# Both directions of a gated linear attention stacked on 128 partitions, with the backward states kept in DRAM

## The chip, the cores and the metric

The kernel runs on one core of a Trainium2 chip. The metric is the device time of one execution in microseconds (us); a kernel's time is the median of its runs. The engines are TensorE (PE; its weight loads are PEld), VectorE (DVE), ScalarE (ACT), GpSimd (POOL) and SyncE (SP), which here only issues DMAs.

## The reference, cut to what matters

One inference step of a two-layer hybrid backbone over 2048 latent tokens and a prompt of 128, model width 1024. The even layer runs a bidirectional gated linear attention (GLA, four heads, 64 key and 128 value channels each) beside a bidirectional S5 scan; the odd layer has windowed attention beside a short convolution. Shift, scale and gate of each layer come from a product with the conditioning vector (adaLN). The GLA of one direction:

```python
def step(S, inp):
    qc, kc, vc, gc = inp
    b = jnp.cumsum(gc, axis=2)
    o_inter = jnp.einsum('bhcd,bhde->bhce', qc * jnp.exp(b), S)
    diff = b[:, :, :, None, :] - b[:, :, None, :, :]
    decay = jnp.where(causal, jnp.exp(jnp.where(causal, diff, 0.0)), 0.0)
    att = jnp.einsum('bhid,bhjd,bhijd->bhij', qc, kc, decay)
    o = o_inter + jnp.einsum('bhij,bhje->bhie', att, vc)
    b_last = b[:, :, -1:, :]
    S_new = jnp.exp(b_last)[:, :, 0, :, None] * S + jnp.einsum('bhcd,bhce->bhde', kc * jnp.exp(b_last - b), vc)
    return S_new, o
```

It is run forward and on the flipped sequence, and both outputs are added: `o_f + fl(o_b)`. Each output chunk thus takes a forward state S (what came before it) and a backward state (what comes after it), each times the queries weighted by that direction's gates.

## The kernel before

Tokens are cut into 17 tiles of 128: 0 to 15 latent, 16 the prompt; a GLA chunk is one such tile. Tensors that pass between stages lie in DRAM (`qk_d`, `v_d`, `b_d` with the cumulated gates of both directions, `ys_d`, `zg_d`). A scheduler that simulates the engines sets the order of instructions on each engine from the program text, so an edit in one place can reorder engines elsewhere. Times are of the profile.

Start, 0 to 60 us. `ada` (L144) makes 512 columns of the adaLN vector: it loads a bias `bb` (L154) and eight weight tiles (L167), multiplies (L170), copies the sum out (L173), adds the bias (L175) and turns it into columns of shift or scale (L185 to L190). Four such units come first. `xt` are the token tiles (L278), `wst` weight tiles (L199) that are split in two parts for products of higher precision, `hf` and `ht` the normalized and modulated tokens and their parts (L245 to L249).

60 to 344 us: input projection (L341, L342) with the setup of S5 beside it. 344 to 715: S5 core, with parts of the projection (`qz_pass`) beside it.

Back stage, 715 to 900. `gla_back` (L890) walks over the tiles from the last to the first and makes every backward state; `zg_pass`, `glu_pass` (L816) and eight more adaLN units run beside it. `kv_update` (L921) turns the weighted keys (L926) and multiplies them with v (L932) for four heads, two on partitions 0 to 63 and two on 64 to 127. All 16 backward states stay in SBUF (`self.sb`, 16 KB per partition).

Crossing and chunks, 900 to 1340. `phase4` (L1132) weaves three chunks in flight: chunk i's attention, the turn of chunk i-1 and the output projection of chunk i-2 (`out_proj`, products into psD). `gla_pre` (L988) loads a chunk and makes `kh` and the queries `hq` weighted by the exponentiated gates (L1012), and steps the forward state (L1031). `gla_arg` (L964) makes the arguments of one of eight levels of the decay: four subtractions on GpSimd (L980 to L983; `q` of the last level on L972), an exponential on ScalarE (L984), a product on VectorE (L985); `gla_chunk` (L1034) multiplies them (L1058) and merges the levels (L1062, L1065). Then come three products per head into one PSUM tile: queries with the forward state (L1073) and with the backward state (L1074), each over 64 rows, and the attention with v (L1075). L1077 copies the result out, L1084 normalizes it.

1340 to 1850: the odd layer's projection and convolution; 1850 to 2422: attention.

Of the kernel before, what the change touches and what calls it, by code (L numbers as in the profile page):

```python
# [48 lines left out]
class Kernel:  # L49
# [55 lines left out]
    def setup(self, es):  # L105
# [33 lines left out]
        self.b_d = d.tile([2, 2, 128, NT], F32, name="b_d")  # L139
        self.z_d = d.tile([16, 512, 137], F32, name="z_d")  # L140
# [3 lines left out]
    def ada(self, l, j, wp, ring=None, bufs=4):  # L144
# [8 lines left out]
        bb = wp.tile([2, n], F32, name="bb", tag="ada_bb", bufs=bufs)  # L153
# [736 lines left out]
    def gla_back(self, es):  # L890

        nc, a = self.nc, self.a
        p = self.pool(es, "gbk", 2, side="left")
        for i in [16] + list(range(15, 0, -1)):
            ts = slice(i * 128, (i + 1) * 128)
            k = p.tile([128, 2, 128], F32, name="bk", tag="bk")
            B = p.tile([128, 2, 128], F32, name="bB", tag="bB")
            nc.sync.dma_start(k, self.qk_d[256:512, ts].rearrange("(r p) t -> p r t", p=128))
            nc.sync.dma_start(B, self.b_d[:, 1, :, ts].rearrange("r p t -> p r t"))
            v = p.tile([128, 512], F32, name="bv", tag="bv")  # L900
            nc.sync.dma_start(v, self.v_d[ts, :])
            E = p.tile([128, 2, 128], F32, name="bE", tag="bE")
            nc.gpsimd.tensor_tensor(E, B[:, :, 0:1].to_broadcast([128, 2, 128]), B, op=OP.subtract)
            nc.scalar.activation(E, E, AF.Exp, scale=0.0625)
            nc.vector.tensor_tensor(E, E, k, op=OP.mult)
            kv = self.kv_update(p, E, v)
            if i == 16:
                st = p.tile([128, 2, 128], F32, name="bst", tag="bst", bufs=1)
                nc.scalar.copy(st, kv)
                nc.sync.dma_start(self.o["gla"][1].rearrange("r p v -> p r v"), st)  # L910
                yield
                continue
            eb = p.tile([128, 2], F32, name="beb", tag="beb")
            nc.scalar.activation(eb, B[:, :, 0], AF.Exp, scale=0.0625)
# [6 lines left out]
    def kv_update(self, p, kd, v):  # L921
# [66 lines left out]
    def gla_pre(self, i):  # L988
# [7 lines left out]
        for j in range(2):  # L996
            nc.sync.dma_start(qk[:, j], self.qk_d[256 * j : 256 * j + 256, ts].rearrange("(r p) t -> p r t", p=128))
            nc.sync.dma_start(B[:, j], self.b_d[:, j, :, ts].rearrange("r p t -> p r t"))
        v = st["v"] = self.ga["v"].tile([128, 512], F32, name="v", tag="v", bufs=1)
# [10 lines left out]
        qh, st["att"] = (qa[:, 512 * j : 512 * j + 512].rearrange("p (a b c) -> p a b c", a=2, b=2) for j in range(2))  # L1010
        st["qh"] = qh
# [9 lines left out]
        sf = st["sf"] = self.sf  # L1021
        if i != 15:
            kv = self.kv_update(p, kh, v)
            if i == 16:
                o = p.tile([128, 2, 128], F32, name="fst", tag="sf", bufs=3)
                nc.scalar.copy(o, kv)
                nc.sync.dma_start(self.o["gla"][0].rearrange("r p v -> p r v"), o)
            else:
                self.sf = p.tile([128, 2, 128], F32, name="sf", tag="sf", bufs=3)
                for pr in range(2):  # L1030
                    V.scalar_tensor_tensor(self.sf[:, pr], sf[:, pr], eb[:, pr : pr + 1], kv[:, pr], op0=OP.mult, op1=OP.add)  # L1031
        yield

    def gla_chunk(self, i, out):  # L1034
# [4 lines left out]
        v, qh, sf = st["v"], st["qh"], st["sf"]  # L1039
# [28 lines left out]
        for h in range(4):  # L1068
            pr, hh = h // 2, h % 2
            o = 64 * hh  # L1070
# [498 lines left out]
    def run(self):  # L1569
        a = self.a  # L1570
        take = lambda g, n: [next(g, None) for _ in range(n)]
        with ExitStack() as es:
            self.setup(es)
            eW = es.enter_context(ExitStack())
            with ExitStack() as eA:
# [21 lines left out]
                c = self.pool(eR, "glac", 1, side="left")  # L1597
                self.sb = c.tile([128, 16, 2, 128], F32, name="sb")
                self.sf = c.tile([128, 2, 128], F32, name="sf0")
                self.nc.sync.dma_start(self.sb[:, 15], a["s0"][1])  # L1600
                self.nc.sync.dma_start(self.sf, a["s0"][0])
# [65 lines left out]
def prep(**z):  # L1667
# [56 lines left out]
        "s0": c_(n["state_gla"][0, 0].reshape(2, 2, 128, 128).transpose(0, 2, 1, 3)),  # L1724
# [51 lines left out]
```

## Time and profile before

| | |
|---|---|
| median of 3 runs | 2425.09 us (2424.18 to 2429.84) |
| profiled execution | 2423.86 us |
| its span | 2422.1 us |
| busy TensorE / VectorE / ScalarE / GpSimd | 2295.5 / 1720.3 / 986.2 / 872.9 us |
| moved by DMA | 303.92 MB |

The span is what the trace covers; the rest of the execution lies around it. Busy times are sums over the span, and TensorE's contains modelled ends. In a row of a timeline, the first number is the start in us, the second the duration of the group in us, `x2` the number of instructions in it; in square brackets stands how long the engine had waited and for what. TensorE's float32 products appear as two records each.

### The profile page before, as it was taken

The page shows a single profiled execution, that of the slowest core. Times are in us where ns is not written, and L with a number is a line of the kernel's source. Part 1 is how long each engine was busy: PE and PEld are TensorE (multiplying, and loading weights), DVE is VectorE, ACT ScalarE, POOL GpSimd, SP SyncE. Part 2 cuts the span into 40 slices and gives each one's busy share as a digit, 9 for nine tenths or more (in the row PEclk, how much of TensorE's full clock was granted, in tenths as well). Part 3 has the DMA queues.
Part 4 walks back from the last instruction along what each step waited for, and adds up shares of the span by engine and source line. Part 5 has one row for each costly group of instructions (what it writes and reads, how often), then busy time and mean ns, then how long its engine had stood idle before and what let it go on. Part 6 is the DMA issues. An engine that isn't in the chain of part 4 may idle for free.

```text
span 2422.1 us, 47150 instructions
## 1 busy us (share of the span) xinstructions
PE 2295.5 (95%) x17521; PEld 2110.7 (87%) x17521; DVE 1720.3 (71%) x3932; ACT 986.2 (41%) x2365; POOL 872.9 (36%) x1328
## 2 busy tenths in 40 slices
PE   7998998999999986999999999999999998999998
PEld 4987887777787875888888999999999997999998
DVE  5998689999976776888888675556344336676765
ACT  4553532222244453445554532233122115565653
POOL 4017047777612227666765022211001102222221
PEclk9999999999999995989999999999999998999999
DMA  8442552233269873333433642245124213222221
GB/s 303 153 141 79 170 159 78 80 82 96 81 202 315 294 242 112 122 105 114 124 118 99 192 135 79 79 134 169 50 73 122 68 56 113 88 88 88 89 70 57
DMA packets 313174, 303.92 MB, mean 125 GB/s; under 512 B 43696, under 2 KB 264464, under 8 KB 312944
## 3 DMA queue, kind: packets, MB, share of 16 engines
q1 hardware_dynamic: 255072, 227.70, 31.6%
q10 hardware_dynamic: 48112, 42.38, 5.4%
q0 software_dynamic: 9760, 30.83, 3.5%
q8 instruction: 138, 2.26, 0.4%
q14 instruction: 92, 0.75, 0.1%
HBM read 212.43 MB, written 88.39 MB: 124 GB/s over the span
## 4 chain that ended last, share of the span: by engine, by line
PE 53%; DVE 7%; issue 5%; DMA 4%; POOL 2%; ACT 2%; SPq 0%; ACTq 0%; POOLq 0%; DVEq 0%
PE psW L100 7%; PE psW L102 7%; PE psW L101 7%; PE psD L100 6%; PE psD L102 6%; PE psD L101 6%; PE psW L1487 2%; PE psW L1440 2%; PE psT L1475 2%; PE psP L1058 2%; PE psP L1075 1%; PE psP L1073 1%; DVE hq L1065 1%; DVE arg L985 1%; DVE yT L1103 1%
## 5 line engine op out<-in xcount | busy, mean ns | idle before, releaser
L100 PE MATMUL psD<-slot,yT 128*128 128x256 f32 x1088 | 316.4, 292 | 2.4 <-ACT yT L1102 2.4
L102 PE MATMUL psD<-slot,yT 128*128 128x256 f32 x1088 | 314.0, 292 | 0.4 <-DVE yT L1103 0.4
L101 PE MATMUL psD<-slot,yT 128*128 128x256 f32 x1088 | 311.2, 287 | 0.0
L101 PE MATMUL psW<-hq,slot 128*128 128x272 f32 x1024 | 293.0, 288 | 0.0
L102 PE MATMUL psW<-hq,slot 128*128 128x272 f32 x1024 | 292.9, 287 | 0.0
L100 PE MATMUL psW<-hq,slot 128*128 128x272 f32 x1024 | 289.1, 287 | 0.0
L101 PE MATMUL psD<-hq,slot 128*128 128x272 f32 x768 | 227.8, 297 | 14.5 <-DVE hq L230 14.5
L100 PE MATMUL psD<-hq,slot 128*128 128x272 f32 x768 | 230.0, 301 | 9.4 <-ACT fo L791 8.2
L102 PE MATMUL psD<-hq,slot 128*128 128x272 f32 x768 | 228.5, 298 | 0.0
L100 PEld LDWEIGHTS psD<-slot,yT 128*128 128x128 f32 x1088 | 208.0, 191 | 9.9 <-ACT yT L1102 2.8
L101 PEld LDWEIGHTS psD<-slot,yT 128*128 128x128 f32 x1088 | 208.1, 191 | 2.1
L102 PEld LDWEIGHTS psD<-slot,yT 128*128 128x128 f32 x1088 | 205.7, 191 | 4.3 <-issue 1.3
L102 PEld LDWEIGHTS psW<-hq,slot 128*128 128x128 f32 x1024 | 193.1, 189 | 0.0
L101 PEld LDWEIGHTS psW<-hq,slot 128*128 128x128 f32 x1024 | 192.5, 188 | 0.0
L100 PEld LDWEIGHTS psW<-hq,slot 128*128 128x128 f32 x1024 | 190.6, 188 | 0.0
L101 PEld LDWEIGHTS psD<-hq,slot 128*128 128x128 f32 x768 | 147.5, 192 | 25.4 <-DVE hq L230 19.2
L100 PEld LDWEIGHTS psD<-hq,slot 128*128 128x128 f32 x768 | 147.9, 193 | 19.5 <-ACT fo L791 10.2
L102 PEld LDWEIGHTS psD<-hq,slot 128*128 128x128 f32 x768 | 147.8, 193 | 8.2 <-issue 8.2
L1449 DVE CUSTOM_DVE_ANT_0 sc<-psW,amask,sink 128x512 f32<-128x512 f32 (+1 forms) x128 | 93.6, 732 | 82.5 <-PE psT L1475 75.3
L984 ACT ACTIVATE arg<-arg 128x512 f32<-128x512 f32 x119 | 75.2, 632 | 134.1 <-POOL arg L983 129.5
L1452 ACT ACTIVATE sc<-sc,nm 128x512 f32<-128x512 f32 (+1 forms) x128 | 90.9, 710 | 85.8 <-DVE nm L1451 71.9
L245 ACT ACTIVATE hf<-psT,msh,msc 128x128 f32<-128x128 f32 x272 | 100.6, 463 | 49.3 <-PE psT L241 49.3
(378 smaller groups left out, 6653.3 us busy)
## 6 DMA issues: line engine op xcount, KB each, us to landing
wst<-h_d SPq DMA_DIRECT2D x136, 272.0 KB
wada<-in_w_ada_dram SPq DMA_DIRECT2D x32, 512.0 KB
h_d<-hf SPq DMA_DIRECT2D x17, 512.0 KB
x_d<-x ACTq DMA_DIRECT2D x17, 512.0 KB
h_d<-hf ACTq DMA_DIRECT2D x17, 512.0 KB
wst<-h_d SPq DMA_DIRECT2D x34, 256.0 KB
qf<-qa_d SPq DMA_DIRECT2D x34, 256.0 KB
hq<-x_d SPq DMA_DIRECT2D x17, 512.0 KB
```

The costliest lines, as they stand in the source:

```text
L100: mm(out, lh, rh, start=start, stop=False)
L101: mm(out, lh, rl, start=False, stop=False)
L102: mm(out, ll, rh, start=False, stop=stop)
L245: nc.scalar.activation(f[:, k, :], pt[:, j, :], AF.Identity, bias=sh, scale=sc)
L984: nc.scalar.activation(arg, arg, AF.Exp, scale=0.0625)
L985: nc.vector.tensor_tensor(arg, arg, qk.rearrange("p j r t -> p j (r t)"), op=OP.mult)
L1058: nc.tensor.matmul(pv[:, hh, pr, :], ak[o : o + 64, pr, :], aq[o : o + 64, pr, :], start=True, stop=True)
L1440: nc.tensor.matmul(out, r32(qs[:, j, h]), kk, start=j == 0, stop=j == 1)
L1449: V.tensor_tensor_reduce(sv, ps, mask, 1.0, sk[:, h : h + 1], op0=OP.add, op1=OP.max, accum_out=m)
L1452: nc.scalar.activation(sv, src, AF.Exp, bias=nm[:, h : h + 1], accum_out=sm[:, h : h + 1])
L1475: nc.tensor.transpose(pt[:, c, :], t[:, 128 * c : 128 * c + 128], self.ident)
L1487: nc.tensor.matmul(po[kv][:, j % 2], r32(VV[:, b, kv]), r32(t[:, x, :, c, :]), start=c + x == 0, stop=c + x == nb)
```

## The change

The two states of a head are stacked: forward on partitions 0 to 63, backward on 64 to 127, one [128, 4, 128] tile for four heads. The queries are stacked the same way: `qq` holds them twice, and `hq` is loaded from `b_d` once more, by direction and head, and exponentiated in place. One product over 128 rows per head then replaces the two over 64. The sum `eb` of the gates, the states' update (`next_state`, a product on GpSimd and an addition on VectorE in place of two fused operations on VectorE) and `kv_update` (all four heads in one half of the partitions) follow that layout. The backward states go to DRAM (`sb_d`) and come back one per chunk (`state`); the pool that held them is gone. `ada` holds half as many bias tiles.

```diff
-        bb = wp.tile([2, n], F32, name="bb", tag="ada_bb", bufs=bufs)
+        bb = wp.tile([2, n], F32, name="bb", tag="ada_bb", bufs=bufs // 2)
...
-            kv = self.kv_update(p, E, v)
+            kv = self.kv_update(p, E, v, 64)
...
-            for pr in range(2):
-                nc.vector.scalar_tensor_tensor(
-                    self.sb[:, i - 1, pr], self.sb[:, i, pr], eb[:, pr : pr + 1], kv[:, pr], op0=OP.mult, op1=OP.add
-                )
+            eb = p.tile([128, 2, 2], F32, name="beb", tag="beb")
+            for hh in range(2):
+                nc.scalar.activation(eb[64:128, :, hh], B[64 * hh : 64 * hh + 64, :, 0], AF.Exp, scale=0.0625)
+            nst = p.tile([128, 4, 128], F32, name="bs", tag="bs", bufs=2)
+            self.next_state(p, slice(64, 128), nst, st, eb, kv)
+            st = nst
+            nc.gpsimd.dma_start(self.sb_d[i - 1], st[64:128])
...
+    def next_state(self, p, o, dst, src, eb, kv):
+
+        t = p.tile([128, 4, 128], F32, name="dst", tag="dst", bufs=1)
+        e = eb.rearrange("p a b -> p (a b)")[o].unsqueeze(2).to_broadcast([64, 4, 128])
+        self.nc.gpsimd.tensor_tensor(t[o], src[o], e, op=OP.mult)
+        self.nc.vector.tensor_tensor(dst[o], t[o], kv, op=OP.add)
...
-        kv = self.bank("T", (128, 2, 128))
+        kv = self.bank("T", (128, 4, 128))[o : o + 64]
         for h in range(4):
-            pr, o = h // 2, 64 * (h % 2)
+            pr, c = h // 2, 64 * (h % 2)
             nc.tensor.matmul(
-                kv[o : o + 64, pr, :],
-                kt[:, pr, o : o + 64],
-                v[:, h * 128 : h * 128 + 128],
-                start=True,
-                stop=True,
-                tile_position=(0, o),
+                kv[:, h], kt[:, pr, c : c + 64], v[:, h * 128 : h * 128 + 128], start=True, stop=True, tile_position=(0, o)
             )
...
-        nc.scalar.activation(qh, B, AF.Exp, scale=0.0625)
-        eb = p.tile([128, 2], F32, name="eb", tag="eb")
-        V.tensor_copy(eb, qh[:, 0, :, 127])
-        V.tensor_tensor(qh, qh, qk[:, 0:1].to_broadcast([128, 2, 2, 128]), op=OP.mult)
+        qh = st["qh"] = qa[:, 0:512].rearrange("p (h c) -> p h c", h=4)
+        if i < 16:
+            qq = p.tile([128, 4, 128], F32, name="qq", tag="qq", bufs=1)
+            for d in range(2):
+                o = slice(64 * d, 64 * d + 64)
+                nc.sync.dma_start(qq[o], self.qk_d[0:256, ts].rearrange("(h k) t -> k h t", k=64))
+                for r in range(2):
+                    nc.sync.dma_start(qh[o, 2 * r : 2 * r + 2], self.b_d[r, d, :, ts].rearrange("(q k) t -> k q t", k=64))
+            nc.scalar.activation(qh, qh, AF.Exp, scale=0.0625)
+            eb = p.tile([128, 2, 2], F32, name="eb", tag="eb")
+            V.tensor_copy(eb[0:64].rearrange("p a b -> p (a b)"), qh[0:64, :, 127])
+            V.tensor_tensor(qh, qh, qq, op=OP.mult)
...
+    def state(self, i):
+
+        self.sf = self.gp.tile([128, 4, 128], F32, name="sf", tag="sf", bufs=3)
+        self.nc.sync.dma_start(self.sf[64:128], self.a["s0"][1] if i == 15 else self.sb_d[i])
...
-                nc.tensor.matmul(ot, qh[o : o + 64, 0, pr, :], sf[o : o + 64, pr], start=True, stop=False)
-                nc.tensor.matmul(ot, qh[o : o + 64, 1, pr, :], self.sb[o : o + 64, i, pr], start=False, stop=False)
+                nc.tensor.matmul(ot, qh[:, h], st["sf"][:, h], start=True, stop=False)
             nc.tensor.matmul(ot, att[:, hh, pr], v[:, h * 128 : h * 128 + 128], start=i == 16, stop=True)
```

The scheduler's order moves in three places that the next section comes to. A row gives the line, the operation, out<-in and the tile's size; lines of the changed kernel are one higher up to about L920 and 6 to 21 higher behind it.

First place: SyncE at the program's start; `bb` is an adaLN bias, `wada` its weights. Before:

```order
L154 DMA bb<-in_b_ada_dram 2x512
L167 DMA wada<-in_w_ada_dram 128x512 x8
L154 DMA bb<-in_b_ada_dram 2x512
L167 DMA wada<-in_w_ada_dram 128x512 x8
L278 DMA xt<-in_xs_dram 128x1024 x2
L154 DMA bb<-in_b_ada_dram 2x512
L167 DMA wada<-in_w_ada_dram 128x512 x12
L154 DMA bb<-in_b_ada_dram 2x512
L167 DMA wada<-in_w_ada_dram 128x512 x4
```

In the changed kernel, further down the same list, the fourth bias load:

```order
L200 DMA wst<-in_w_in_e_dram 128x512
L324 DMA w2f<-in_gla_w_dram 16x256 x6
L328 DMA b_122<-in_gla_b_dram 128x4
L329 DMA rmask<-in_rmask_dram 128x256
L200 DMA wst<-in_w_in_e_dram 128x544
L200 DMA wst<-in_w_in_e_dram 128x512
L279 DMA xt<-in_xs_dram 128x1024 x4
L155 DMA bb<-in_b_ada_dram 2x512
L200 DMA wst<-in_w_in_e_dram 128x544
```

The fourth bias stood behind the first two `xt` loads and 28 `wada`, ahead of every `wst`; now it stands behind ten `wst` loads and the group of four `xt`.

Second place: VectorE at the start; `ba<-ba,bb` is the bias added (the third and the fourth of four), `rsv`, `rsy` and `rst` belong to the reciprocal root of the norm. Before:

```order
L173 COPY ba<-psW 128x512
L175 TENSOR_TENSOR ba<-ba,bb 2x512
L188 COPY msh_74<-psT 128x8
L173 COPY ba<-psW 128x512
L175 TENSOR_TENSOR ba<-ba,bb 2x512
L190 SCALAR_TENSOR_TENSOR msc_72<-psT,nw 128x8
L247 CAST ht<-hf 128x512 x2
L249 TENSOR_TENSOR ht<-hf,ht 128x1024
L326 TENSOR_TENSOR w_119<-w2f,w_119 32x512
```

In the changed kernel:

```order
L176 TENSOR_TENSOR ba<-ba,bb 2x512
L189 COPY msh_74<-psT 128x8
L327 TENSOR_TENSOR w_120<-w2f,w_120 32x512
L89 TENSOR_SCALAR rsv<-ss_124 128x2
L90 TENSOR_SCALAR rsy<-rsv 128x2
L92 SCALAR_TENSOR_TENSOR rst<-rsy 128x2
L93 TENSOR_TENSOR rst<-rst,rsv 128x2
L94 SCALAR_TENSOR_TENSOR rsy<-rst,rsy 128x2
L92 SCALAR_TENSOR_TENSOR rst<-rsy 128x2
L93 TENSOR_TENSOR rst<-rst,rsv 128x2
L94 SCALAR_TENSOR_TENSOR rsy<-rst,rsy 128x2
L176 TENSOR_TENSOR ba<-ba,bb 2x512
```

The last addition, and with it the last columns of the scale (`msc`), moved from ahead of the first `ht` to behind eight operations of the norm of the next tokens.

Third place: GpSimd's list around the crossing from the GLU stage to the chunks; `ys_d<-gzs` and `zg_d<-fo` are stores of the stage before, `kh` and `arg` belong to chunk 0. Before:

```order
L866 DMA ys_d<-gzs 128x272 x3
L812 DMA zg_d<-fo 128x272
L866 DMA ys_d<-gzs 128x272
L1005 TENSOR_TENSOR kh<-B 128x256
L980 TENSOR_TENSOR arg<-B 128x8x16
L981 TENSOR_TENSOR arg<-B 128x8x16
L982 TENSOR_TENSOR arg<-B 128x8x16
L983 TENSOR_TENSOR arg<-B 128x8x16
```

In the changed kernel:

```order
L922 DMA sb_d<-bs 64x512
L813 DMA zg_d<-fo 128x272
L1016 TENSOR_TENSOR kh<-B 128x256
L986 TENSOR_TENSOR arg<-B 128x8x16
L987 TENSOR_TENSOR arg<-B 128x8x16
L988 TENSOR_TENSOR arg<-B 128x8x16
L989 TENSOR_TENSOR arg<-B 128x8x16
L867 DMA ys_d<-gzs 128x272
L986 TENSOR_TENSOR arg<-B 128x16x8
L987 TENSOR_TENSOR arg<-B 128x16x8
L988 TENSOR_TENSOR arg<-B 128x16x8
L989 TENSOR_TENSOR arg<-B 128x16x8
```

and at the last of the stores:

```order
L813 DMA zg_d<-fo 128x272
L867 DMA ys_d<-gzs 128x272 x3
L813 DMA zg_d<-fo 128x272
L867 DMA ys_d<-gzs 128x272
L986 TENSOR_TENSOR arg<-B 128x2x64
L987 TENSOR_TENSOR arg<-B 128x2x64
L988 TENSOR_TENSOR arg<-B 128x2x64
L989 TENSOR_TENSOR arg<-B 128x2x64
```

Chunk 0's `kh` and its first levels moved ahead of most stores; behind the last store (`L867`) stand levels of chunk 1, and chunk 0's last level soon after.

## Rows read from the trace of the kernel before

**Rows 1.** Length, busy us of PE, PEld, DVE, ACT, POOL; clock, DMA share, GB/s.

```profile
200.00:344.00 144.00, 128.49 (x847) 115.94 (x846) 109.02 (x180) 67.95 (x155) 51.40 (x76) 0.94 0.52 151
344.00:720.00 376.00, 343.75 (x2389) 298.12 (x2388) 343.23 (x684) 105.35 (x391) 243.09 (x313) 0.97 0.35 98
720.00:900.00 180.00, 177.43 (x1354) 147.38 (x1353) 126.29 (x265) 92.14 (x214) 48.75 (x84) 1.00 0.90 293
900.00:960.00 60.00, 35.66 (x212) 28.87 (x211) 39.80 (x79) 23.59 (x50) 41.87 (x80) 0.63 0.39 122
1100.00:1310.00 210.00, 209.15 (x1732) 182.54 (x1731) 181.28 (x424) 106.64 (x263) 149.84 (x274) 1.00 0.38 117
```

**Rows 2.** The chain of waits, 909 to 924: start us, us, what.

```profile
909.33 3.51 DMA ys_d<-gzs
913.23 1.15 POOL kh L1005
...
922.81 1.14 POOL q L972
```

**Rows 3.** Timeline of TensorE, two heads of one chunk: start us, us, instructions.

```profile
1115.49 0.49 PE L1073 MATMUL psP<-sf,hq 64*128 64x128 f32 x2
1115.81 0.38 PE L1074 MATMUL psP<-sb,hq 64*128 64x128 f32 x2
1116.12 0.49 PE L1075 MATMUL psP<-v,hq 128*128 128x128 f32 x2
1116.54 0.48 PE L1073 MATMUL psP<-sf,hq 64*128 64x128 f32 x2
```

**Rows 4.** Timeline of TensorE in the S5 core: products of 137 columns.

```profile
547.27 0.40 PE L714 MATMUL psW<-s5U,tz 128*128 128x137 f32 x2
547.50 0.40 PE L715 MATMUL psW<-s5U,tz 128*128 128x137 f32 x2
```

**Rows 5.** Timeline of TensorE in the back stage: kv_update's products.

```profile
812.56 0.66 PE L932 MATMUL psT<-bv,kt 128*64 128x128 f32 x8
813.15 0.44 PE L926 MATMUL psT<-ident,bE 128*128 128x128 f32 x2
```

**Rows 6.** All instructions of L1077: min/median/max ns, first and last start.

```profile
L1077 DVE COPY gy<-psP x17: 680/691/692, 945.4 to 1335.2; 128x512 f32<-128x512 f32 x17
```

**Rows 7.** All instructions of L1084 and of L1031.

```profile
L1084 POOL TENSOR_TENSOR gy<-gy,rsy x17: 1041/1042/1407, 954.4 to 1343.8; 128x512 f32<-128x512 f32 x17
L1031 DVE SCALAR_TENSOR_TENSOR sf<-sf,eb,psT x30: 328/334/342, 923.3 to 1263.0; 128x128 f32<-128x128 f32 x30
```

**Rows 8.** Timeline of SyncE's queue at the start.

```profile
38.13 1.85 SPq L278 DMA_DIRECT2D xt<-in_xs_dram  x4
```

**Rows 9.** Timeline of ScalarE at the start, with its wait.

```profile
48.59 0.65 ACT L200 CAST w1h<-wst 128x544 fp32r<-128x544 f32 x1 [0.81 <-DMA wst<-in_w_in_e_dram]
```

**Rows 10.** Timeline of VectorE at the start.

```profile
32.46 1.44 DVE L175 TENSOR_TENSOR ba<-ba,bb 2x512 f32<-2x512 f32 x1
...
50.93 1.27 DVE L93 TENSOR_TENSOR rst<-rst,rsv 128x2 f32<-128x2 f32 x1
```

**Rows 11.** Timeline of TensorE at the start.

```profile
42.91 0.82 PE L341 MATMUL psW<-w1h,ht 128*128 128x272 f32 x2 [2.02 <-DVE ht L249]
...
59.03 0.33 PE L241 MATMUL psT<-ident,xt 128*128 128x128 f32 x1 [2.08 <-DVE xt L283]
```

**Rows 12.** Timeline of VectorE, two casts of one size.

```profile
207.85 13.38 DVE L247 CAST ht<-hf 128x512 fp32r<-128x512 f32 x1 [1.40 <-ACT hf L245]
...
223.72 0.42 DVE L247 CAST ht<-hf 128x512 fp32r<-128x512 f32 x1
```

**Rows 13.** Timeline of TensorE, first heads of chunk 0.

```profile
936.85 0.79 PE L1073 MATMUL psP<-sf,hq 64*128 64x128 f32 x2 [0.99 <-DVE hq L1065]
...
939.67 0.79 PE L1073 MATMUL psP<-sf,hq 64*128 64x128 f32 x2
```

**Rows 14.** Timeline of ScalarE, the exponential of one chunk.

```profile
1095.88 0.63 ACT L1012 ACTIVATE hq<-B 128x512 f32<-128x512 f32 x1 [1.59 <-PE psP L1075]
```

More of the change, by code (lines that the diff above doesn't have):

```diff
@@ L139, in setup @@
         self.b_d = d.tile([2, 2, 128, NT], F32, name="b_d")
+        self.sb_d = d.tile([15, 64, 4, 128], F32, name="sb_d")
         self.z_d = d.tile([16, 512, 137], F32, name="z_d")
@@ L905, in gla_back, with kv_update @@
             nc.vector.tensor_tensor(E, E, k, op=OP.mult)
-            kv = self.kv_update(p, E, v)
+            kv = self.kv_update(p, E, v, 64)
             if i == 16:
-                st = p.tile([128, 2, 128], F32, name="bst", tag="bst", bufs=1)
-                nc.scalar.copy(st, kv)
-                nc.sync.dma_start(self.o["gla"][1].rearrange("r p v -> p r v"), st)
+                fin = p.tile([128, 4, 128], F32, name="bs", tag="bs", bufs=2)
+                nc.scalar.copy(fin[64:128], kv)
+                nc.sync.dma_start(self.o["gla"][1].rearrange("r (q k) v -> k (r q) v", q=2), fin[64:128])
+                st = p.tile([128, 4, 128], F32, name="bs", tag="bs", bufs=2)
+                nc.sync.dma_start(st[64:128], a["s0"][1])
                 yield
                 continue
-            eb = p.tile([128, 2], F32, name="beb", tag="beb")
-            nc.scalar.activation(eb, B[:, :, 0], AF.Exp, scale=0.0625)
-            for pr in range(2):
-                nc.vector.scalar_tensor_tensor(
-                    self.sb[:, i - 1, pr], self.sb[:, i, pr], eb[:, pr : pr + 1], kv[:, pr], op0=OP.mult, op1=OP.add
-                )
-            yield
-    def kv_update(self, p, kd, v):
+            eb = p.tile([128, 2, 2], F32, name="beb", tag="beb")
[5 more added lines that the diff above has]
+            nc.gpsimd.dma_start(self.sb_d[i - 1], st[64:128])
+            yield
+    def next_state(self, p, o, dst, src, eb, kv):
[3 more added lines that the diff above has]
+        self.nc.vector.tensor_tensor(dst[o], t[o], kv, op=OP.add)
+    def kv_update(self, p, kd, v, o):
         nc = self.nc
@@ L998, in gla_pre @@
             nc.sync.dma_start(B[:, j], self.b_d[:, j, :, ts].rearrange("r p t -> p r t"))
+        if i < 16:
+            if i == 0:
+                self.state(0)
+                nc.sync.dma_start(self.sf[0:64], a["s0"][0])
+            st["sf"] = self.sf
         v = st["v"] = self.ga["v"].tile([128, 512], F32, name="v", tag="v", bufs=1)
@@ L1009, in gla_pre @@
         qa = self.ha.tile([128, 2, 2, 272], F32, name="hq", tag="hq").rearrange("p a b c -> p (a b c)")
[L1010 to L1015 removed]
+        st["att"] = qa[:, 512:1024].rearrange("p (a b c) -> p a b c", a=2, b=2)
+        qh = st["qh"] = qa[:, 0:512].rearrange("p (h c) -> p h c", h=4)
+        if i < 16:
+            qq = p.tile([128, 4, 128], F32, name="qq", tag="qq", bufs=1)
[8 more added lines that the diff above has]
+            V.tensor_tensor(qh, qh, qq, op=OP.mult)
         yield
@@ L1020, in gla_pre @@
         yield
-        sf = st["sf"] = self.sf
         if i != 15:
-            kv = self.kv_update(p, kh, v)
+            kv = self.kv_update(p, kh, v, 0)
             if i == 16:
-                o = p.tile([128, 2, 128], F32, name="fst", tag="sf", bufs=3)
-                nc.scalar.copy(o, kv)
-                nc.sync.dma_start(self.o["gla"][0].rearrange("r p v -> p r v"), o)
-            else:
-                self.sf = p.tile([128, 2, 128], F32, name="sf", tag="sf", bufs=3)
-                for pr in range(2):
-                    V.scalar_tensor_tensor(self.sf[:, pr], sf[:, pr], eb[:, pr : pr + 1], kv[:, pr], op0=OP.mult, op1=OP.add)
+                o = p.tile([128, 4, 128], F32, name="fst", tag="dst", bufs=1)
+                nc.scalar.copy(o[0:64], kv)
+                nc.sync.dma_start(self.o["gla"][0].rearrange("r (q k) v -> k (r q) v", q=2), o[0:64])
+            else:
+                self.state(i + 1)
+                self.next_state(p, slice(0, 64), self.sf, st["sf"], eb, kv)
         yield
+    def state(self, i):
+        self.sf = self.gp.tile([128, 4, 128], F32, name="sf", tag="sf", bufs=3)
+        self.nc.sync.dma_start(self.sf[64:128], self.a["s0"][1] if i == 15 else self.sb_d[i])
     def gla_chunk(self, i, out):
@@ L1596, in run @@
                 eR = es.enter_context(ExitStack())
[L1597 to L1601, printed above, removed]
                 with ExitStack() as e1:
```

5 lines of the change are left out of this document (2 added, 3 removed).

## The prediction

> **What bounds the kernel now.** I read the table of stretches first, since the engine that leads differs from stage to stage. Each of its rows has a stretch, its length, and what each engine is busy in it. In the back stage (720 to 900 us) TensorE is busy 177.43 of 180 us, with a DMA share of 0.90; in the GLA chunks (1100 to 1310) TensorE 209.15 of 210 and VectorE 181.28 [rows 1]. So what TensorE is spared there comes off the time, until VectorE or the chain of one chunk takes over. From 344 to 720 us VectorE leads with 343.23 of 376, and TensorE has 32 us of room. From 900 to 960 us nothing leads by much: TensorE is busy 35.66 of 60 at a granted clock of 0.63, and GpSimd 41.87 [rows 1]. The chain of waits, read next, shows why: GpSimd starts chunk 0's first subtraction at 913.23 us, behind a store of ys_d, and then works without a gap [rows 2]. The timelines of single engines, read last, give the durations below.
>
> **The change, part by part.** The sum is made against the profiled execution: 2423.9 us (span 2422.1, with 1.8 outside it), 1.2 below the median of 2425.1.
>
> *One product per head, chunks.* A head's three products run at 1115.49 (L1073), 1115.81 (L1074) and 1116.12 us (L1075), and the next head starts at 1116.54: 0.32 + 0.31 + 0.42 = 1.05 us, 4.2 us a chunk [rows 3]. Afterwards there are two products a head, both of 128 rows by 128 columns of the array. What such a pair costs this trace doesn't show in place. From below: in the S5 core, products of the same shape with 137 columns start 0.23 us apart (547.27, 547.50) [rows 4], so 128 columns take 0.22, a head 0.44 and a chunk 1.76, which saves 2.4. From above: L1075 has that shape too and costs 0.42 [rows 3]; then a head is 0.84, and a chunk saves 0.8. I take 0.22, since L1075 stands between products on half of the rows and those in the S5 core do not, and afterwards neither does any of these. For 16 chunks that is 39 us (13 from above).
>
> *kv_update.* Today the four heads' products write two column groups in turn: 8 records at 812.56, and the next instruction at 813.15, so 0.59 us [rows 5]. Now all four write one group (forward 0, backward 64). Bounds: no change; or eight records that follow each other as the half-row ones of L1074 do, 0.31 us per two, 1.24 in all [rows 3]. I take 1.1, near the upper end, as neither row shows overlap on one group: +0.5 us for each of 32 updates, 16 in the back stage (+8, bounds 0 to +11) and 16 in the chunks (+8). The Trainium skill ("TensorEngine Tiling (Array Packing)", Key Properties) says that different tiles can load and multiply in parallel, which speaks against this edit; by a full loss of that overlap each update would take 1.18 us, and the 32 together 19 us rather than my 16. The order on one group is shown by no run here.
>
> *Chunks, sum.* A chunk takes (1335.2 - 945.4)/16 = 24.4 us [rows 6]. TensorE is spared 2.4 - 0.5 = 1.9 of them, 31 in 16 chunks. VectorE works 181.28/210 of the time [rows 1], 21.0 us a chunk, and does as much as before: the state's update was two operations of a third of a us (L1031 [rows 7]) and becomes one addition of 64x512 out of PSUM, like L1077's 0.69 us [rows 6]. At 22.5 us a chunk VectorE would be 93% busy, so I count two thirds: **-21** (bounds -6, with the dearer products, and -39).
> What the chunks gain in work: on GpSimd a product of 64x512 each (at most L1084's 1.04 us for 128x512 [rows 7]; its load is 149.84 of 210 us, 17.4 of 24.4, so it stays under TensorE); on the queues seven loads, 640 KB, for each of 16 chunks, some 10 MB beside 117 GB/s at a DMA share of 0.38 [rows 1]. I cost both at nothing as long as that room is left. The exponential of the stacked gates now reads tiles that its own four loads fill; that is the slower rival below.
>
> *Back stage.* Besides kv_update: 15 stores of 128 KB into a DMA share of 0.90, and the bias tile of the adaLN units held once instead of twice, so SyncE's queue stands at a bias load until the unit before has added, and the h and zs loads stand behind it. TensorE waits 2.6 us of 180 today, so cover exists; bounds 0 and +9, of which I take none. **+8** stays, from kv_update.
>
> *Start.* With one bias tile where there were two, the fourth adaLN unit's bias can be loaded only once the third has used it, and the order puts it behind four xt loads. These were issued at 38.13 us for 1.85 us [rows 8]; a weight tile issued behind them landed at 48.59, where ScalarE waited for it [rows 9]. So the addition that ran at 32.46 us [rows 10] runs at 49 or later, and on VectorE it stands behind eight operations of the rsqrt chain, of which some take 1.27 us beside GpSimd's work [rows 10]: up to 10 us more. Until it is done no column of the scale is there, no hf, no ht, and TensorE's first products (42.91 us, released by ht [rows 11]) wait: about 10.4 us behind the addition as today, 59 to 69. Of 16 to 26 us of delay, transposes and the 2.08 us wait at 59.03 [rows 11], which will be over by then, take some back; I put the lag at 16. Behind it TensorE has 15.5 us of room from 200 to 344 and 32 beyond [rows 1], of which I let it use 6: **+10** (bounds 0, all absorbed, and +18).
> On the lengthened operations: the CAST of ht takes 13.38 us at 207.85 and 0.42 at 223.72 [rows 12]. The Trainium skill ("SBUF — State Buffer", SBUF: two separate sides) explains such a pair: VectorE and GpSimd share a port that one locks for a whole instruction; the trace agrees (13.38 against 0.42). By that rule GpSimd's new state products lock VectorE out, which is a rival below.
>
> *Crossing.* GpSimd's list of chunk 0 was kh, four levels of arg (16 operations) and q, all behind the last ys_d stores, 913.23 to 923.95 us [rows 2]; now they stand ahead of most of these stores, and after the last store come only the levels of chunk 1 and chunk 0's last. That frees 10.7 us, and the 3.5 for which kh waited on the store [rows 2]: up to 14. TensorE's own order then takes over. The heads come at a low clock there, 2.8 us for the first (936.85 to 939.67 [rows 13]), and I let them start near 924. **-14** (bounds -3 and -20, the latter with the clock back earlier).
>
> Sum: -21 + 8 + 10 - 14 = -17. 2423.9 - 17 = 2407 on the profiled execution's scale; with the 1.2 that the median lies above it, I say 2408.
>
> **Rivals.**
> *A, VectorE takes over in the chunks.* For: 181.28 of 210 us. Against: it waits for TensorE at L1077 today. Gain there 10 instead of 21: 2419.
> *B, slower: the exponential waits for its loads.* Before, ScalarE did it at 1095.88, released by TensorE's last product of the chunk before [rows 14], on data long there. Now that product frees the tile, then four loads are issued (1.85/4 = 0.46 us each [rows 8]) and land (3.5 us, as the ys_d store did [rows 2]): about 5.4 us, with the later exponentials of arg behind it in ScalarE's order. For: the chunk's levels are a chain through ScalarE. Against: the order puts the exponential behind the squares and the first copy, and ScalarE is busy half of the time (106.64 of 210 [rows 1]). It decides from a stall of (17 + 7)/16 = 1.5 us per chunk; at half, 2.7, the time is 2408 + 43 = 2451.
> *C, the late start is absorbed* by the S5 core, which VectorE leads: 2398.
> *D, 128-row products stay at 0.42 us*, and the change does not do what it says: chunks save 13 - 8 = 5, two thirds of it 3, instead of 21: 2426.
> *E, the port.* Each state product holds VectorE up for up to 1.04 us, 17 in 16 chunks [rows 7]: the chunk gain falls to 4: 2425.
>
> **How the numbers follow.** Forecast 0.44 (own range 2398 to 2418), A 0.14, B 0.12, C 0.12, D 0.12, E 0.06. The range reaches down to C with the upper crossing gain and up past D and E to a small stall of B: 2388 to 2432. What a measurement can tell from no change is 0.3%, 7.3 us: faster is under 2418, slower over 2432. Faster: forecast nearly all (0.42), C 0.12, A half (0.07), D a little (0.02): 0.63. Same: the rest of A and D, and E: 0.22. Slower: B, and D or E with the late start in full: 0.15.
>
> **What would show it.** Right: two products of a head starting 0.22 apart; the copies of gy out of PSUM (L1097 there) 22.5 to 23 us apart, the first of them near 930; TensorE's first product of the input projection near 60 us; the records of kv_update taking about 1.1 us. Wrong: ScalarE idle before the exponential with a gate load as releaser and arg late behind it (B); VectorE busy over 95% from 960 to 1310 (A, E); 0.42 between the products (D); SyncE standing at a bias load in the back stage while TensorE waits for h.

## The result: slower by 0.7%

| | before | changed |
|---|---|---|
| median | 2426.8 us (4 runs, 2424.2 to 2429.8) | 2443.8 us (4 runs, 2442.1 to 2447.2) |
| ratio | | 1.0071 [1.0057, 1.0086] |
| span of the profiled execution | 2422.1 | 2440.7 |

The forecast was 2408. I follow the span from milestone to milestone: the start of the S5 core's last product (called its end), the start of the last GLU product, the start of the first and of the last copy of gy (L1077, now L1097), the end.

| up to | before | changed | longer by | forecast |
|---|---|---|---|---|
| S5 core's end | 714.1 | 724.0 | +9.9 | +10 |
| last GLU product | 901.7 | 923.7 | +12.1 | +8 |
| first copy of gy | 945.4 | 957.1 | -10.3 | -14 |
| last copy of gy | 1335.2 | 1356.7 | +9.8 | -21 |
| end of span | 2422.1 | 2440.7 | -2.9 | 0 |

The first three lines have the sign and about the size of the forecast, and the last is small. The chunks missed by 31 us, of the 36 by which the time missed.

The changed kernel by stretches (columns as in [rows 1]):

```profile
720.00:900.00 180.00, 171.84 (x1268) 144.12 (x1268) 124.61 (x221) 89.51 (x214) 80.15 (x126) 0.99 0.88 283
1100.00:1310.00 210.00, 190.29 (x1576) 172.62 (x1575) 185.01 (x396) 97.93 (x251) 140.68 (x261) 0.94 0.45 134
```

In the chunks TensorE is busy 190.29 of 210 us, no longer 209.15 [rows 1]: its work went, and it now waits for others. The granted clock was lower too, 0.94 where it had been 1.00. VectorE is at 185.01, not at its limit either. No engine leads; so the reader has to look for a chain.

TensorE's timeline in one chunk, against [rows 3]:

```profile
1128.46 1.09 PE L943 MATMUL psT<-v,kt 128*64 128x128 f32 x8
1129.48 0.39 PE L100 MATMUL psD<-slot,yT 128*128 128x256 f32 x1
...
1130.40 0.39 PE L1094 MATMUL psP<-sf,hq 128*128 128x128 f32 x2
1130.62 0.39 PE L1095 MATMUL psP<-v,hq 128*128 128x128 f32 x2
1130.85 0.39 PE L1094 MATMUL psP<-sf,hq 128*128 128x128 f32 x2
```

A product takes 0.22 us and a head 0.45 (was 1.05), so what TensorE was to be spared it was spared. kv_update takes 1.02 us, where [rows 5] had 0.59.

What TensorE waits for begins on SyncE, ScalarE and GpSimd. SyncE's queue after the end of a chunk:

```profile
1107.96 3.10 SPq L1030 DMA_DIRECT2D hq<-b_d  x4
```

ScalarE, with the wait in brackets (answers to [rows 14]):

```profile
1113.48 0.63 ACT L1031 ACTIVATE hq<-hq 128x512 f32<-128x512 f32 x1 [2.32 <-DMA hq<-b_d]
1114.02 1.13 ACT L990 ACTIVATE arg<-arg 128x512 f32<-128x512 f32 x2
```

GpSimd a moment later:

```profile
1115.41 2.09 POOL L929 TENSOR_TENSOR dst<-sf,eb 64x512 f32<-64x512 f32 x1 [1.42 <-DVE eb L1033]
1117.46 0.41 POOL L986 TENSOR_TENSOR arg<-B 128x128 f32<-128x128 f32 x1
```

The loads of the stacked gates can be issued only when the chunk before has given up its hq tile; the exponential waits for them, with the exponentials of arg behind it; eb needs that exponential, and the state's product on GpSimd needs eb, with the subtractions of the next level behind it. All of these stand at the head of the chain of levels.

How much in all, by the waits of the changed kernel from 975 to 1345 us (total, times, longest):

```profile
ACT hq L1031 <- DMA hq<-b_d: 34.8, 13, 4.0
```

by GpSimd's groups of instructions from 960 to 1345 us (busy and mean ns, then idle time before and what ended it):

```profile
L929 POOL TENSOR_TENSOR dst<-sf,eb 64x512 f32<-64x512 f32 x13 | 14.9, 1146 | 14.0 <-DVE rsy L94 5.0 <-DVE eb L1033 3.3 <-DVE rst L92 2.7
```

and by VectorE's, from 960 to 1330, the changed kernel and then the one before:

```profile
L991 DVE TENSOR_TENSOR arg<-arg,qk 128x512 f32<-128x512 f32 x102 | 96.7, 949 | 20.6 <-ACT arg L990 20.4
```

```profile
L985 DVE TENSOR_TENSOR arg<-arg,qk 128x512 f32<-128x512 f32 x101 | 80.8, 801 | 19.5 <-ACT arg L984 19.4
```

The mean of L991 hides a few long ones that begin just behind the state's product. VectorE's timeline at one of them,

```profile
1243.57 3.66 DVE L991 TENSOR_TENSOR arg<-arg,qk 128x512 f32<-128x512 f32 x1 [0.17 <-ACT arg L990]
```

and GpSimd's:

```profile
1243.41 1.03 POOL L929 TENSOR_TENSOR dst<-sf,eb 64x512 f32<-64x512 f32 x1 [1.89 <-DVE rsy L94]
1244.41 0.41 POOL L986 TENSOR_TENSOR arg<-B 128x128 f32<-128x128 f32 x1
...
1246.26 0.42 POOL L987 TENSOR_TENSOR arg<-B 128x128 f32<-128x128 f32 x1
1246.65 0.84 POOL L988 TENSOR_TENSOR arg<-B 128x128 f32<-128x128 f32 x1
1247.45 0.84 POOL L989 TENSOR_TENSOR arg<-B 128x128 f32<-128x128 f32 x1
```

GpSimd begins 0.16 us ahead and goes on without a gap, at 0.41 us an operation; VectorE's product, 0.69 us elsewhere, ends only at 1247.23, while one of GpSimd's takes 0.84.

So there are 34.8 us of waiting for the gate loads on ScalarE, 28.9 on GpSimd (14.9 of work, 14.0 of standing), and 15.9 us more in VectorE's products of arg. These overlap; what each is worth is for experiments.

### The profile page after: what moved, and what is told of

The parts are those of the page before. It is cut to its first block, busy times and chain, and to the rows that moved or that the text cites. A ratio compares the mean times of both kernels' runs of the same rounds, so it can differ in the third digit from the quotient of the medians.

```text
span 2440.7 us, 47173 instructions
## 1 busy us (share of the span) xinstructions
PE 2274.5 (93%) x17393; PEld 2107.3 (86%) x17393; DVE 1741.7 (71%) x3900; ACT 983.8 (40%) x2379; POOL 913.7 (37%) x1373
## 4 chain that ended last, share of the span: by engine, by line
PE 49%; DVE 8%; issue 6%; DMA 5%; POOL 2%; ACT 2%; SPq 1%; ACTq 0%; DVEq 0%; POOLq 0%
PE psW L100 7%; PE psW L101 7%; PE psW L102 7%; PE psD L100 5%; PE psD L101 5%; PE psD L102 5%; PE psW L1507 2%; PE psW L1460 2%; PE psT L1495 2%; DMA hq<-b_d 1%; PE psP L1080 1%; DVE arg L991 1%; PE psT L943 1%; DVE hq L1087 1%; DVE yT L1123 1%
## 5 line engine op out<-in xcount | busy, mean ns | idle before, releaser
L100 PE MATMUL psD<-slot,yT 128*128 128x256 f32 x1088 | 319.7, 295 | 1.4 <-ACT yT L1122 1.3
L102 PE MATMUL psD<-slot,yT 128*128 128x256 f32 x1088 | 317.0, 294 | 1.0 <-DVE yT L1123 1.0
L101 PE MATMUL psD<-slot,yT 128*128 128x256 f32 x1088 | 315.7, 291 | 0.0
L100 PE MATMUL psD<-hq,slot 128*128 128x272 f32 x768 | 229.4, 300 | 11.6 <-ACT fo L792 8.2
L100 PEld LDWEIGHTS psD<-slot,yT 128*128 128x128 f32 x1088 | 211.0, 194 | 7.7 <-issue 2.2
L101 PEld LDWEIGHTS psD<-slot,yT 128*128 128x128 f32 x1088 | 211.1, 194 | 3.8 <-issue 0.6
L102 PEld LDWEIGHTS psD<-slot,yT 128*128 128x128 f32 x1088 | 209.5, 194 | 4.5 <-DVE yT L1123 1.2
L1080 PE MATMUL psP<-arg 64*128 64x128 f32 x952 | 92.0, 318 | 41.7 <-DVE rst L93 14.3
L991 DVE TENSOR_TENSOR arg<-arg,qk 128x512 f32<-128x512 f32 x119 | 113.4, 956 | 21.3 <-ACT arg L990 21.0
```

The costliest lines, as they stand in the source:

```text
L100: mm(out, lh, rh, start=start, stop=False)
L101: mm(out, lh, rl, start=False, stop=False)
L102: mm(out, ll, rh, start=False, stop=stop)
L991: nc.vector.tensor_tensor(arg, arg, qk.rearrange("p j r t -> p j (r t)"), op=OP.mult)
L1080: nc.tensor.matmul(pv[:, hh, pr, :], ak[o : o + 64, pr, :], aq[o : o + 64, pr, :], start=True, stop=True)
```

## The experiments

All times are medians, ratios against runs of the kernel before on the same chip. "Chunks" is the time from the first to the last copy of gy in the profiled execution: 389.8 us before, 399.6 changed. That is one execution, and its time can lie off the median: by 14 us in the changed kernel with added TensorE work, 13 of them before the S5 core's end. Each edit also gives the scheduler another order, which by itself moves this number by several us (the two runs on the bias tile below: -6 and -8.5).

**Own tile for the gate loads** (on the changed kernel)

```diff
+            bq = p.tile([128, 4, 128], F32, name="bq", tag="bq", bufs=1)
...
-                    nc.sync.dma_start(qh[o, 2 * r : 2 * r + 2], self.b_d[r, d, :, ts].rearrange("(q k) t -> k q t", k=64))
-            nc.scalar.activation(qh, qh, AF.Exp, scale=0.0625)
+                    nc.sync.dma_start(bq[o, 2 * r : 2 * r + 2], self.b_d[r, d, :, ts].rearrange("(q k) t -> k q t", k=64))
+            nc.scalar.activation(qh, bq, AF.Exp, scale=0.0625)
```

> The changed kernel, but the four gate loads of a chunk go to a tile of their own, which is free as soon as the exponential of the chunk before has read it; the exponential writes hq from there. Loads, bytes, products and kv_update stay. Theory W (the exponential waits behind loads that can only be issued once the chunk before has released hq; ScalarE's later work waits behind it): the waits for hq<-b_d (34.8 us in 13) go, first to last copy of gy takes 360 to 372 us where the changed kernel takes 399.6, time 2443.8 - 30 to 40, so 2404 to 2414. Rival T (640 KB of loads per chunk, or GpSimd's state products holding VectorE, slow the chunks): these are all still there, so first to last copy stays at 390 or more and the time at 2434 or more.

2430.6 us, 1.0017 [1.0006, 1.0029]; chunks:

```profile
L1098 DVE COPY gy<-psP x17: 671/678/692, 954.4 to 1337.8; 128x512 f32<-128x512 f32 x17
```

383.4, 16 less (the time fell by 13), with every load still there. The late loads count, at half of what I expected; the traffic alone does not explain the loss, and something besides the wait has a part in it. VectorE's products of arg, from 960 to 1330 us in this run:

```profile
L991 DVE TENSOR_TENSOR arg<-arg,qk 128x512 f32<-128x512 f32 x105 | 84.6, 807 | 18.0 <-ACT arg L990 18.0
```

The long ones behind the state's product are gone, 807 ns on average against 949, although GpSimd still has that product. In the changed kernel the exponential of the gates and two of arg ran one behind the other once the loads had landed (1113.48 and 1114.02 us above), so that the state's product and VectorE's began together. That the late loads brought the two together is read from these rows and not tested by itself; the 16 us can hold both, the wait and the hold on VectorE.

**The wait alone, in the kernel before**

```diff
-        nc.scalar.activation(qh, B, AF.Exp, scale=0.0625)
+        for j in range(2):
+            for r in range(2):
+                nc.sync.dma_start(qh[:, j, r], self.b_d[r, j, :, ts])
+        nc.scalar.activation(qh, qh, AF.Exp, scale=0.0625)
```

> The kernel before, with only the wait added: the gates that the exponential reads are loaded once more per chunk by four loads into hq itself, in the old layout, and exponentiated in place (256 KB more per chunk; no stacking, no state in DRAM, all products as before). Theory W: ScalarE waits some 2.5 us per chunk for these loads, and as the chunk's levels pass through ScalarE, first to last copy of gy grows from 389.8 by 20 to 40 us; time 2447 to 2467. Rival (ScalarE is busy half of the time, so such a wait is covered): 2427 to 2430, with ScalarE's wait in the trace all the same.

2426.8, 1.0008 [0.9998, 1.0018]; chunks 390.2 (946.4 to 1336.6). A miss. ScalarE waited, as the waits of this run show,

```profile
ACT hq L1015 <- DMA hq<-b_d: 19.5, 13, 2.1
```

and nothing came of it. But the exponential had waited before the edit as well, for TensorE's last product of the chunk before; the waits of the kernel before, from 960 to 1335 us:

```profile
ACT hq L1012 <- PE psP L1075: 31.3, 10, 7.9
```

So the edit put a shorter wait in the place of a longer one, and the run does not tell what a longer one costs. The changed kernel's 34.8 us are hardly more than these 31.3 either. What is new there is what hangs on the exponential: GpSimd's state product needs its result, and in the old kernel no GpSimd work does.

**The state's product on ScalarE** (on the changed kernel)

```diff
-        e = eb.rearrange("p a b -> p (a b)")[o].unsqueeze(2).to_broadcast([64, 4, 128])
-        self.nc.gpsimd.tensor_tensor(t[o], src[o], e, op=OP.mult)
+        e = eb.rearrange("p a b -> p (a b)")
+        for h in range(4):
+            self.nc.scalar.activation(t[o, h], src[o, h], AF.Identity, scale=e[o, h : h + 1])
```

> The changed kernel with the state's product on ScalarE (four operations of 64x128 with a scale per partition) in place of GpSimd's, in the back stage and in the chunks. Theory E: VectorE's product of arg (949 ns on average in the changed kernel, 801 before) falls back towards 801, first to last copy of gy falls from 399.6 to 385 to 390, time 2429 to 2436. In the back stage GpSimd's queue of stores runs freer: the last GLU product up to 4 us earlier. Rival (the wait of the exponential explains it all): 2440 to 2447.

2428.0, 1.0008 [0.9998, 1.0017]; chunks:

```profile
L1098 DVE COPY gy<-psP x17: 672/675/692, 967.2 to 1339.9; 128x512 f32<-128x512 f32 x17
```

372.7, 27 less, and VectorE's product of arg falls to 819 ns. The exponential's wait is still there (34.5 us in 13). This is the larger of the two causes, larger than theory E had it. Taking the product off GpSimd takes away its hold on VectorE and its standing in GpSimd's list for eb alike; this run doesn't part the two. The back stage was longer with it: the last GLU addition 216 us after the S5 core's end, not 207.

**Both** (one bias tile as changed)

> The changed kernel with the own tile for the gate loads and the state's product on ScalarE, one bias tile as changed. Fourth corner beside the changed kernel (first to last copy 399.6), the own tile (383.4) and ScalarE's product (372.7): if the two waits add, 356 to 366 and a time of 2410 to 2416, the late start of 7 to 10 us being still in it; if one stood for the other, 372 or more and 2424 or more.

2424.1, 0.9996 [0.9981, 1.0011]; chunks 964.3 to 1333.9, 369.6. The two overlap: 16 and 27 alone, 30 together. Against the own tile alone it is 14 less, with VectorE's products already back at 807 ns there: so most of these 14 are not the hold on VectorE, but the product's work and its place in GpSimd's list.

**One more GpSimd product in the kernel before**

```diff
+                t = p.tile([128, 4, 128], F32, name="dst", tag="dst", bufs=1)
+                G.tensor_tensor(t[0:64], qh[0:64].rearrange("p a b c -> p (a b) c"), eb[0:64, 0:1].unsqueeze(2).to_broadcast([64, 4, 128]), op=OP.mult)
```

> The kernel before with one more product of 64x512 on GpSimd in each chunk (into a tile that nothing reads), where the changed kernel has its state product. Theory E (GpSimd's product holds VectorE at the shared port, and GpSimd's list gets longer): VectorE's products L985 get longer (801 ns on average now), first to last copy of gy grows by 6 to 16 us, time 2432 to 2442. Rival (GpSimd's room covers it): 389.8 +- 3, time 2426.

2431.5, 1.0022 [1.0011, 1.0033]; chunks 945.0 to 1339.3, 394.3 (+4.5). The product has a price of its own, but VectorE's L985 did not get longer on average (772 ns): in this place, and with nothing waiting for its result, it holds VectorE up less than in the changed kernel.

**The bias tile**: two of them again in the changed kernel (`bufs=bufs`), and one in the kernel before (`bufs=bufs // 2`).

> The changed kernel with two bias tiles again where it has one. Theory: the first product of the input projection is at 43 us where the changed kernel has 59, the S5 core ends near 713 where it has 723, and the time falls by 10 to 2434. If the bias tile also costs in the back stage (SyncE stands at a bias load), the last GLU product comes 4 us earlier still, 2430. Rival (VectorE or the loads pace the start, the bias is incidental): 2444, no change.

> The kernel before with one bias tile where it has two, nothing else. Theory: the first product of the input projection moves from 43 to 59 us, the S5 core's end by 10 us, and 8 to 10 of these reach the end: 2426.8 + 9 = 2436. If the back stage loses by the bias too: 2440. Rival (absorbed): 2427.

Two in the changed kernel: 2436.4, 1.0045 [1.0032, 1.0058], 7 less; S5 core's end 713.4. One in the old kernel: 2428.1, 1.0017 [1.0009, 1.0026]; its first product of the input projection

```profile
59.23 0.82 PE L341 MATMUL psW<-w1h,ht 128*128 128x272 f32 x2 [5.69 <-DVE ht L247]
```

as in the changed kernel, S5 core's end 723.4, and the first copy of gy still 11.6 later; then the chunks took 383.4 and gave 6 back. In the changed kernel with two tiles the start was 10.6 us earlier, but the first copy of gy only 1.8 (955.3), and the chunks took 391.1, 8.5 less. The delay at the start is shown; how much of it reaches the end depends on what follows, and the 7 us are not simply a part of it.

**Is TensorE's time worth anything in a chunk?** Four runs: L1074 left out of the kernel before, and 128 products added (each of a head's products with the state issued three times, into the same place) to the kernel before, to the changed kernel, and to the one with three edits (below).

```diff
-                nc.tensor.matmul(ot, qh[:, h], st["sf"][:, h], start=True, stop=False)
+                for n in range(3):
+                    nc.tensor.matmul(ot, qh[:, h], st["sf"][:, h], start=True, stop=n < 2)
```

> The kernel before without the product of the queries with the backward state (L1074, 64 products in 16 chunks left out, so their part of the output is missing; nothing else). It asks what TensorE time is worth in a chunk at all. Premise of the forecast (TensorE bounds the chunks): 4 x 0.31 = 1.25 us a chunk, 20 us in 16; first to last copy of gy 389.8 - 15 to 20 = 370 to 375, time 2426 - 15 to 20. Rival (a chunk is a chain through GpSimd, ScalarE, VectorE and TensorE, and TensorE's other products only fill it): TensorE idles instead, first to last copy 383 to 390, time 2418 to 2426.

> The kernel before with the forward product (L1073) issued three times into the same place: 128 products more, the counterpart of leaving L1074 out. If the old chunks have two bounds close together, leaving out gives nothing and adding costs nearly in full: two products of 0.2 to 0.3 us, four heads, 16 chunks, 26 to 41 us, first to last copy 412 to 430, time 2448 to 2466. If the chain alone sets the pace and TensorE has room: 390 to 398, time 2426 to 2434.

> The changed kernel with each head's stacked product (L1094) issued three times into the same place, so that the result stays and TensorE has 128 products of 0.22 us more: 1.78 us per chunk, 28 us in all, about what the change took away. Theory K (a chunk's pace is set by the chain through GpSimd, ScalarE, VectorE and TensorE, and TensorE has 39 us of idle time between these copies): first to last copy of gy 399.6 + 0 to 10, time 2444 to 2454. Rival P (TensorE's time counts one for one, as the forecast had it): 428, time 2472.

> The same 128 extra products in the kernel with the three edits (own tile, two bias tiles, state's product on ScalarE; 2407.7, first to last copy 365.1). If TensorE's time counts once the chain is shorter: 385 to 393, time 2427 to 2436, so that the merged products are worth most of their 31 us there. If the chain still sets the pace: 365 to 372, time 2408 to 2415.

| kernel | TensorE work | time | ratio | chunks |
|---|---|---|---|---|
| before | -20 us | 2427.6 | 0.9998 [0.9984, 1.0012] | 395.8 |
| before | +29 us | 2448.8 | 1.0086 [1.0070, 1.0102] | 410.3 |
| changed | +28 us | 2446.4 | 1.0092 [1.0070, 1.0114] | 398.3 |
| three edits | +28 us | 2427.0 | 1.0003 [0.9994, 1.0011] | 385.2 |

(The 29 come from six records of L1074 there taking 0.77 us where two took 0.32.) In the changed kernel 28 us of TensorE's time cost 2.6 us (5 by the ratios), and its chunks not one; TensorE was busy 375.25 of their 398.3 us, so it was not their limit. In the old kernel taking 20 away gave nothing, and adding 29 cost 22. That fits old chunks at two limits at once, TensorE's list and the chain of levels, of which the change relieved the first and lengthened the second. But the granted clock, here a mean of its levels of 1.2 and 2.4 GHz, moved along: over the chunks it fell from 0.95 to 0.92 without L1074, and TensorE's busy time by 3.6 us (379.47 to 375.89) instead of 20; with the added products in the changed kernel it rose from 0.93 to 0.98, and the busy time by 15 (from 360.28) instead of 28. So a part of the spared work can have gone into the lower clock instead; these runs do not part the two readings.

**Old kernel, ScalarE's wait relieved**: own tile for the exponentiated gates, two buffers, then three, then three and without L1074.

```diff
+        qh = st["qh"] = self.ge.tile([128, 2, 2, 128], F32, name="qh", tag="qh", bufs=2)
```

> The kernel before with a tile of its own (two buffers) for the exponentiated gates, so that ScalarE's exponential no longer waits for TensorE's last product of the chunk before (31.3 us in 10 waits). If waits in ScalarE's order set the pace of the chunks there too: first to last copy of gy 389.8 - 5 to 15, time 2411 to 2421. If TensorE's products do (209 of 210 us busy): 387 to 392, time 2424 to 2428.

> The kernel before with three buffers of its own for the exponentiated gates, so that the exponential is not held by the product of an earlier chunk (with two buffers 26.3 us of that wait were left). If TensorE bounds the old chunks: first to last copy of gy 387 to 392, time 2424 to 2428. If ScalarE's wait does: 375 to 385, 2411 to 2421.

> The same, and without the product of the queries with the backward state (left out: 20 us of TensorE time, and that part of the output). Theory of two bounds that lie close together (TensorE's list and the chain through ScalarE; either one alone relieved gives nothing, as the kernel before without L1074 showed): together first to last copy 370 to 378, time 2406 to 2414. Rival (TensorE's time is worth nothing in the old chunks whatever ScalarE does): as the run beside it, within 4 us.

Two: 2427.7, 1.0007 [0.9996, 1.0019], the wait still there (26.3 us), so this tells nothing. Three: 2441.6, 1.0062 [1.0048, 1.0076]; the exponential now stood in wait for B's load (24.0 us). Three without L1074: 2422.9, 0.9994 [0.9983, 1.0006], chunks 386.2 against 398.0; the time is 19 less than with L1074, so in this order the 20 us of TensorE's time count nearly in full. Moving that exponential forward in ScalarE's list was no relief, so which wait forms the old chain is not settled by these.

**Three edits together**: own tile, two bias tiles, state's product on ScalarE.

> The changed kernel with three edits together: gate loads in a tile of their own, two bias tiles, the state's product on ScalarE. By the sums of the single runs (13 less, 7 less, and some 8 for the state) 2443.8 - 28 = 2416, below the kernel before (2425.6). If one of them only stood in for another: 2425 to 2432.

2407.7, 0.9918 [0.9904, 0.9933]: faster than both. Its stretch in the chunks and its copies:

```profile
1100.00:1310.00 210.00, 203.12 (x1731) 181.02 (x1731) 186.02 (x432) 112.61 (x297) 136.37 (x260) 1.00 0.45 137
```

```profile
L1099 DVE COPY gy<-psP x17: 672/676/692, 949.8 to 1314.9; 128x512 f32<-128x512 f32 x17
```

Chunks 365.1, 25 less than before, TensorE busy again and its clock at 1.00. Added TensorE work costs 20 of 28 there (385.2): TensorE's time counts again once less holds the chunk. That the merged products gain as much there is not shown, since these edits were not run with unmerged ones. The state's product on GpSimd again in the back stage only:

> The kernel with the three edits, but with the state's product on GpSimd again in the back stage, where ScalarE's four operations went with a longer stage (last GLU addition 216 us after the S5 core's end with them in the changed kernel, 206 without). Chunks as in the kernel with three edits (365). If ScalarE was in the back stage's way: that stage 200 to 206 us instead of 212, time 2398 to 2403. If not: 2405 to 2411.

2412.3, 0.9939 [0.9920, 0.9958]; last GLU product 919.5 against 917.9. With two bias tiles ScalarE was not what made the back stage longer: from the S5 core's end to the last GLU addition it took 213.4 us here, 213.7 with three edits, and 214.1 in the changed kernel with two bias tiles alone. With one bias tile this is open: 216.4 and 213.9 with the product on ScalarE, 206.6 and 206.2 on GpSimd.

## Why the prediction was wrong, step by step

*Start (+10): right.* The fourth addition ran at 47.16 us (I had 49 or later), the first product of the input projection at 59.18, and the S5 core ended 9.9 later. One reading behind it was wrong: from 344 to 720 us VectorE does not lead, TensorE is busy 343.75 of 376 us beside its 343.23 [rows 1]. The time that the bias tile was worth varied: 2.5 us in the old kernel, 7 in the changed one, 16 between both edits with one bias tile (2424.1) and with two (2407.7).

*Back stage (+8): mechanism right, size short, +12.1.* kv_update's records take 17.4 us instead of 10.5 there, 0.43 each (I took 0.5). The Trainium skill's rule on tiles that work in parallel ("TensorEngine Tiling (Array Packing)", Key Properties) pointed the right way: 1.02 us is most of the 1.18 of a full loss. The other 5 us I had put at nothing; TensorE waited 8.0 us between the S5 core's end and the last GLU product, not 2.6. 3.3 of these ended with VectorE's `fo` (L812) and 2.1 with ScalarE's `gzh` (L848), against 1.2 and 0.2 before; why these came late stays open.

*Crossing (-14): sign right, -10.3, the mechanism only in part.* GpSimd's list moved as forecast (`kh` of chunk 0 at 891.23 us). But the first head came at 955.15 us, 31.4 behind the last GLU product, where it had come 35.1 behind it: 3.7 us gained, not 13. VectorE waited for the `qq` loads, issued on SyncE from 936.97 us, and in TensorE's list products into psD, released by VectorE's `yT` at 950.79, stood ahead of the heads. The other 6.6 us I had not counted on, and that they fill up most of the term is luck: behind those products the four heads, now two products each, ran at a granted clock of 1.00 (2.4 GHz) and took 2.0 us to the copy, where they had taken 8.6 at 0.50 (1.2 GHz; 936.8 to 945.4 us, [rows 13]).

*Chunks (-21): wrong, +9.8.* Two steps failed. First "what TensorE is spared there comes off the time": the prediction named the chain of one chunk as what would take over, and gave it no price. In the changed kernel TensorE was spared that time and stood idle for 20 of 210 us, and 28 us more of its work cost 2.6. Second, what the chunks gain in work was cost "at nothing as long as that room is left": GpSimd had room on average (140.68 of 210), but the product stood where the next level waited behind it and where VectorE's product began beside it, and cost up to 27 us of chunks; the gate loads, a term that I had left to rival B, up to 16, both 30. With both taken off, the chunks took 369.6 us, 20 less than before and about the -21 of the forecast. The price of the merged product was as forecast (0.22), so rival D fell; A did too, VectorE being busy 185 of 210.

*Rivals.* B was the slower one: its mechanism is there (2.7 us a time, just the half I worked out), but taking the late loads away gave 16 us back, not 43. I had counted its waits from nothing, and the old exponential had waited 31.3 us as well, for TensorE. E is there too, and I gave it 0.06 and 17 us; on ScalarE instead, the product gave 27 us of chunks back. How much of that is the port stays open: with the own tile VectorE's long products went, and GpSimd's state product stayed. The trace agrees with the Trainium skill ("SBUF — State Buffer", SBUF: two separate sides), by which either engine can hold the port they share for a whole instruction, in that one VectorE product took 3.66 us beside GpSimd's; here it was held for longer than one instruction, through several of GpSimd's.

## What to carry to other kernels

Time that a change spares the busiest engine of a stage is gained only until another chain takes over: before counting it as time, ask what the next instructions wait for if that engine were free. Adding work to it and taking work away are two cheap runs; they can differ, and the granted clock has to be read beside them. A wait that a trace shows is to be compared with the wait that stood in its place before. Work that is moved to an engine with room on average costs by its place in that engine's list: look at what it waits for and at what stands behind it. A load into a tile that another stage still holds can only be issued late; a small tile of its own lets it come early.

## Not expected of the hardware

The granted clock of the chunks (1100 to 1310 us) did not go by TensorE's busy time alone: it was 0.94 at 190.29 us busy of 210 in the changed kernel, but 0.99 at 193.12 with the own tile, 0.95 at 200.25 without L1074, and 1.00 at 203.12 (three edits) and 209.15 (before). What else decides it stays open. A product of 128 by 128 rows and columns with 128 columns of data cost 0.42 us between products over half the rows [rows 3] and 0.22 among its like.
